# A hybrid trunk step on one core: spreading products, tile scaling, casts, first taps and score copies are placed differently

## The chip, the cores and the metric

The kernel runs on one core of a Trainium2 chip. A core has five engines, each with its own queue of instructions that runs in order: TensorE (PE, with its weight loads listed as PEld), VectorE (DVE), ScalarE (ACT), GpSimd (POOL) and SyncE (SP), which here only issues transfers. The metric is the device time of one launch in microseconds. Three runs of the kernel before took 1754.55, 1755.26 and 1755.8 us; the median is 1755.26 us.

## The reference

One layer of a hybrid trunk over 128 context and 256 latent tokens of width 2048, all in float32:

```python
mod = (jax.nn.silu(cond) @ p['w_mod'] + p['b_mod'])[:, None, :]
sh1, sc1, g1, sh2, sc2, g2 = jnp.split(mod, 6, axis=-1)
h = _rmsnorm(x, p['ln1_g']) * (1 + sc1) + sh1
z = h @ p['w_in']
q, k, v, cva, cvg, lx, lg = jnp.split(z, IN_SPLITS, axis=-1)
...
mix = jnp.concatenate([att.reshape(B, S, D_ATT), cv, rec], axis=-1) @ p['w_out']
x = x + g1 * mix
h = _rmsnorm(x, p['ln2_g']) * (1 + sc2) + sh2
u = _dwconv(h @ p['ffn_up'], p['ffn_conv_w'], p['ffn_conv_b'], FFN_CONV_WIDTH // 2, FFN_CONV_WIDTH // 2)
ug, uv = jnp.split(u, 2, axis=-1)
x = x + g2 * ((jax.nn.silu(ug) * uv) @ p['ffn_down'])
```

`att` is attention with 8 heads of 128 (context tokens read context; latent tokens read a window of latents with a bias, and a cached context). `cv` is a gated depthwise convolution of 31 taps with a LayerNorm and SiLU, `rec` a recurrence in two directions behind a convolution of 4 taps. A final RMSNorm ends the step.

## The kernel before, in words

**Products.** Every float32 matrix product is made of three products of rounded parts (`mm3`, L161 to L165): a weight piece of 128x1024 is loaded (`raw`), rounded on ACT (`whi`, L150), and the rest is taken on DVE (`wlo`, L152). There are 6 `raw` buffers and 3 each of `whi` and `wlo`. Sums of the large products go to 5 PSUM buffers (`mm_ps`), all others to 3 (`aux_ps`).

**The start** (`in_proj`, L529). x arrives transposed as 16 k-tiles of 128x384. Its squares are summed (`mean_squares`, products msq L505), and `norm_x` (L509) makes the factor 1/rms of each token: a sum and an addition on DVE, a power on POOL (L515), three diagonal matrices on DVE (L520), and three spreading products on PE (rx, L522) that put the factor of every token into all partitions. `scale(k, n)` (L523, L525) multiplies n k-tiles by it on DVE, reading rx. The modulation of a group of k-tiles comes from `mod_pair` (L244): products of w_mod chunks with the condition (modp, L271), a copy on ACT (L331), a transpose (modt, L334) and three or more small DVE operations into MC (L339 to L349). `modulate` (L471) then applies MC on ACT (`ht`, L477), rounds the tile on DVE (`hh`, L479) and takes the rest on DVE (`hl`, L480).

The k-tiles go in groups of 1, 1, 2, 4, 4 and 4 (`GROUPS`, numbered g = 0 to 5). In each group `proj_group` (L564) makes 20 output tiles; the first group's sums are copied on ACT (L584), later ones are added to z on DVE (L586), which also frees their PSUM buffer. The modulation of the next group runs beside it. For the groups that start at k-tile 8 and 12 (`mod_quad`, L279) a part is summed on DVE (L298, L300). In the kernel before, k-tile 0 is scaled at L537, and k-tiles 1 to 15 right behind the last operation of k-tile 0's `modulate` (`issue_after`, L549 to L551), in pieces of 3, 4, 4 and 4. `setup2` (L206, called in group 2) holds a short chain on DVE and one exponential on ACT (L214 to L230).

**Streams.** From `qkv` on, side work is cut into generators (`attention`, `conv_module`, `recurrent`, `mod_*`) that yield costs. Main products call `turn`, which advances each stream by its own rate; for attention it is 3.5 units for each 7.8 us of main work (AR, UNIT). `attention` (L677) for one head: mask (LAG0), then three score blocks, each of products S (L692 to L697), a scaled copy on DVE (L700 or L702 and L703), the maximum on DVE (L705), the exponential on ACT (L706), a reciprocal on DVE (L707) and a scaling on ACT (L708). Then it yields LAG1, transposes the blocks on PE (PTp, L719), copies them on ACT (L722, L724), multiplies by V (o, L727, L729) and copies the result on ACT (L731). `mod_cols` (L399) yields LAG1 too, between a copy and its transposes. `out_proj` (L867) drains what is left of the attention before its products with k-tiles 4 to 7 of the mixed heads (L886).

**Who sets the order.** The program's order gives priorities; a scheduler at build time places each engine's instructions by them and by what it takes to be ready, and may bring an instruction far forward. `high_priority` puts a block first, and `issue_after(i)` keeps a block's instructions on i's engine behind i.

Of the kernel before, what the change touches and what calls it, by code (L numbers as in the profile page):

```python
# [10 lines left out]
AF = mybir.ActivationFunctionType  # L11
ALU = mybir.AluOpType
# [11 lines left out]
SCALE = float(128 ** -0.5)  # L24
NEG = -1e30
CTX = 128
LAT = 256
T = CTX + LAT
TP = T + 2
NSLOT = 54  # L30
RAWB, HLB, MB, MMB, AUXB = 6, 3, 9, 5, 3
GROUPS = (1, 1, 2, 4, 4, 4)
# [8 lines left out]
CR, CV, AR = 2.5, 6, 3.5  # L41
MOD0, MOD1, MOD2 = 2.6, 1.3, .25

LAG0, LAG1, LAG2, LAG3 = 1, 1, 2, 3

RINGS = 4096

# [52 lines left out]
class Trunk:  # L100
# [140 lines left out]
        nc.gpsimd.dma_start(self.G[:, 3072:4096], I["cache_k"])  # L241


    def mod_pair(self, k0, kt):  # L244

        nc, tc = self.nc, self.tc
        pm = self.aux_ps("modp")
        parts = 1 if kt == 1 else 2
        w = kt * P // parts
        nk = 4 // kt  # L250
        wm = self.I["w_mod"]
        chunks = []
        n = KT // nk
        ends = bursts(n) if kt > 1 else list(range(1, n + 1))
        done = 0
        for i in range(n + PLAG):
            if i < n:
                v = self.misc("rawm")
                nc.sync.dma_start(v, wm[4 * k0 + i])
                chunks.append(v.rearrange("p (v k c) -> p v k c", v=2, k=nk))  # L260
                yield nk / KT
            if i + 1 - PLAG in ends:

                with tc.high_priority():
                    for m in reversed(range(done, i + 1 - PLAG)):
                        for k in range(nk):
                            for j in range(2 * parts):
                                vv, half = divmod(j, parts)
                                if parts == 1:
                                    j += 2 * (k % 2)  # L270
                                self.pair = nc.tensor.matmul(  # L271
                                    pm[32 * j:32 * j + 32, :w], lhsT=self.cT[:, m * nk + k, :],
                                    rhs=chunks[m][:, vv, k, half * w:(half + 1) * w],
                                    start=m == ends[0] - 1 and k < 3 - parts, stop=m == ends[-2] and k > nk - 4 + parts)
                done = i + 1 - PLAG
        with tc.high_priority():
            self.mod_pair_cols(k0, kt, w, parts, pm)

# [189 lines left out]
            self.hold = ins  # L468
        return hi, lo

    def modulate(self, kt, x, a, b):  # L471

        nc = self.nc
        t = self.slot(T, "ht")
        hi, lo = self.slot(T, "hh", F32R), self.slot(T, "hl", F32R)
        for c, s0, s1 in SEG:
            nc.scalar.activation(t[:, s0:s1], x[:, s0:s1], AF.Identity, bias=self.MC[:, b, kt, c:c + 1],  # L477
                                 scale=self.MC[:, a, kt, c:c + 1])
        nc.vector.tensor_copy(hi, t)  # L479
        return hi, lo, nc.vector.tensor_tensor(lo, t, hi.bitcast(F32), ALU.subtract)  # L480


# [26 lines left out]
    def norm_x(self, X, pm):  # L509

        nc = self.nc
# [12 lines left out]
            x = X[:, k:k + n]  # L524
            return nc.vector.tensor_tensor(x, x, r.unsqueeze(1).broadcast_to([P, n, T]), ALU.mult)  # L525

        return scale

    def in_proj(self):  # L529
        nc, tc = self.nc, self.tc  # L530
        st = self.streams
        X = self.load_x()
        pm = self.mean_squares(X)
        st.add("pair", 0, self.mod_pair(0, GROUPS[0]))
        st.drain("pair")
        scale = self.norm_x(X, pm)
        scale(0, 1)  # L537
        self.z = {}
        self.h = []
        k0 = 0  # L540
        for g, kt in enumerate(GROUPS):
            with tc.high_priority():
                for k in range(k0, k0 + kt):
                    *h, ins = self.modulate(k, X[:, k], 1, 0)
                    self.h.append(h)
            if g == 0:

                self.hold = self.scaled = ins
                with tc.issue_after(ins.ins):  # L549
                    for k, n in ((1, 3), (4, 4), (8, 4), (12, 4)):  # L550
                        scale(k, n)  # L551
            if g == 2:
                mark = self.mp.tile([P, 2], F32, tag="mark", bufs=1, name="mark")
                with tc.issue_after(nc.gpsimd.tensor_copy(mark, self.MC[:, 0, k0, :]).ins):
# [122 lines left out]
    def attention(self, h):  # L677
# [8 lines left out]
        for i in range(3):  # L686
# [10 lines left out]
                nc.tensor.matmul(o[:, LAT:T], lhsT=ql, rhs=self.ckT[:, h, :], start=True, stop=True)  # L697
            s = self.slot(n, "s")
            if i == 0:
                nc.vector.tensor_scalar(s, S[:, :n], SCALE, None, ALU.mult)  # L700
            else:
                nc.vector.scalar_tensor_tensor(s[:, :LAT], S[:, :LAT], SCALE, bt[i - 1][:, ::-1], ALU.mult, ALU.add)  # L702
                nc.vector.tensor_scalar(s[:, LAT:], S[:, LAT:T], SCALE, None, ALU.mult)  # L703
            st = self.mp.tile([P, 4], F32, tag="st", bufs=6, name="st")
            nc.vector.tensor_reduce(st[:, 0:1], s, AX.X, ALU.max, negate=True)  # L705
            nc.scalar.activation(s, s, AF.Exp, bias=st[:, 0:1], accum_out=st[:, 1:2])  # L706
# [29 lines left out]
    def conv_module(self):  # L736
# [7 lines left out]
        for c in range(4):  # L744
            a, g = self.z[24 + c], self.z[28 + c]
            u = self.mp.tile([P, W], F32, tag="cu", bufs=2, name="cu")
            nc.vector.memset(u, 0.0)
            nc.vector.tensor_tensor(u[:, 15:15 + CTX], a[:, :CTX], g[:, :CTX], ALU.mult)
            nc.vector.tensor_tensor(u[:, 30 + CTX:30 + T], a[:, CTX:], g[:, CTX:], ALU.mult)
            acc = self.slot(N, "cacc")  # L750
            nc.vector.tensor_scalar(acc, u[:, 0:N], self.cvw[:, c:c + 1], self.cv_b[:, c:c + 1], ALU.mult, ALU.add)
            yield 1.0
            for w in range(1, 31):
                nc.vector.scalar_tensor_tensor(acc, u[:, w:w + N], self.cvw[:, 4 * w + c:4 * w + c + 1], acc,  # L754
# [37 lines left out]
    def recurrent(self):  # L792
# [4 lines left out]
        for c in range(4):  # L797
            x = self.z[32 + c]
            u = self.mp.tile([P, TP + 3], F32, tag="cu", bufs=2, name="lu")
            nc.vector.memset(u, 0.0)  # L800
            nc.scalar.copy(u[:, 2:2 + CTX], x[:, :CTX])
            nc.scalar.copy(u[:, 4 + CTX:4 + T], x[:, CTX:])
            xc = self.slot(TP, "xc")
            nc.vector.tensor_scalar(xc, u[:, 0:TP], self.lcw[:, c:c + 1], self.lcb[:, c:c + 1], ALU.mult, ALU.add)
            for w in range(1, 4):
                nc.vector.scalar_tensor_tensor(xc, u[:, w:w + TP], self.lcw[:, 4 * w + c:4 * w + c + 1], xc,
                                               ALU.mult, ALU.add)
# [414 lines left out]
```

## Time and profile before

| | us |
|---|---|
| median of 3 runs | 1755.26 |
| the profiled execution's own time | 1755.48 |
| its span, from first to last instruction | 1753.7 |
| TensorE busy | 1718.2 |
| VectorE busy | 1160.9 |
| ScalarE busy | 741.9 |
| GpSimd busy | 146.0 |

The profiled execution is one run; some 1.8 us lie outside its span. "Busy" counts an instruction from its start to its end; matmuls overlap in a pipeline, so that PE can be busy and still not at its peak. All times below are from the start of the span. Of the granted clock, 1.00 is TensorE's upper level of 2.4 GHz, and 0.50 the lower one of 1.2 GHz.

### The profile page before, as it was taken

The numbers are of one execution on the slowest core, as the hardware profiler recorded it, in microseconds if no ns is written. First come the engines' busy times: TensorE is split into PE (matmuls) and PEld (weight loads), VectorE is DVE, ScalarE is ACT, GpSimd is POOL, SyncE is SP. The second block draws the span as 40 slices with busy tenths as digits, with TensorE's granted clock in tenths as the row PEclk, the third lists the DMA queues.
The fourth block names the chain that finished last, engine by engine and source line by source line (L and its number), as shares of the span: only waits on it lengthen the run. The fifth ranks groups of instructions, "written<-read, shape, count | busy, mean of one in ns | idle before, by whom it ended". The sixth has DMA issues, their size and how long they took to land.

```text
span 1753.7 us, 25229 instructions
## 1 busy us (share of the span) xinstructions
PE 1718.2 (98%) x9935; PEld 1559.9 (89%) x9935; DVE 1160.9 (66%) x1663; ACT 741.9 (42%) x1176; POOL 146.0 (8%) x240
## 2 busy tenths in 40 slices
PE   6999999999999989999999999999999999999998
PEld 5789988779887989999989898998989899898987
DVE  5699799988697455569544545459754545448467
ACT  5223456774443335443424343342434333333434
POOL 0100101313522000001000000001000000000002
PEclk9999999999999999999999999999999999999999
DMA  9887869898687443347444343447434343644333
GB/s 380 300 312 286 230 212 285 252 329 284 141 275 265 152 171 122 126 151 252 144 126 127 120 133 120 133 139 242 135 121 132 113 137 124 234 134 126 123 127 112
DMA packets 192839, 325.57 MB, mean 186 GB/s; under 512 B 11360, under 2 KB 123872, under 8 KB 192208
## 3 DMA queue, kind: packets, MB, share of 16 engines
q1 hardware_dynamic: 179136, 277.97, 47.0%
q0 software_dynamic: 13440, 45.94, 10.1%
q8 instruction: 78, 1.28, 0.3%
q14 instruction: 41, 0.34, 0.1%
q10 hardware_dynamic: 144, 0.05, 0.0%
HBM read 316.54 MB, written 7.38 MB: 185 GB/s over the span
## 4 chain that ended last, share of the span: by engine, by line
PE 92%; DVE 3%; issue 2%; ACT 1%; DMA 1%; POOL 0%; DVEq 0%; SPq 0%; POOLq 0%; ACTq 0%
PE mmp L163 29%; PE mmp L165 28%; PE mmp L164 28%; PE modp L367 1%; PE modp L271 1%; DVE wlo L152 1%; DVE acc L390 1%; DMA rawm<-w_mod 1%; ACT whi L150 0%; PE modp L396 0%; DVE acc L300 0%; PE o L729 0%; PE modp L306 0%; DMA X<-x_T 0%; PE PTp L719 0%
## 5 line engine op out<-in xcount | busy, mean ns | idle before, releaser
L152 DVE TENSOR_TENSOR wlo<-raw,whi 128x1024 fp32r<-128x1024 f32 x371 | 451.5, 1221 | 439.5 <-ACT whi L150 435.1
L150 ACT CAST whi<-raw 128x1024 fp32r<-128x1024 f32 x371 | 387.6, 1047 | 651.8 <-PE mmp L164 351.8
L163 PE MATMUL mmp<-hh,whi 128*128 128x384 f32 x1904 | 645.9, 341 | 6.7 <-DVE hh L479 3.5
L164 PE MATMUL mmp<-hl,whi 128*128 128x384 f32 x1904 | 642.4, 338 | 0.5 <-DVE hl L480 0.5
L165 PE MATMUL mmp<-hh,wlo 128*128 128x384 f32 x1904 | 642.5, 338 | 0.0
L163 PEld LDWEIGHTS mmp<-hh,whi 128*128 128x128 f32 x1904 | 357.8, 188 | 15.3 <-DVE hh L479 4.4
L164 PEld LDWEIGHTS mmp<-hl,whi 128*128 128x128 f32 x1904 | 358.5, 188 | 4.2 <-issue 2.4
L165 PEld LDWEIGHTS mmp<-hh,wlo 128*128 128x128 f32 x1904 | 358.4, 188 | 3.7 <-issue 2.0
L164 PE MATMUL mmp<-wlo,gh 128*128 128x512 f32 x504 | 198.8, 394 | 0.0
L165 PE MATMUL mmp<-whi,gl 128*128 128x512 f32 x504 | 198.4, 394 | 0.0
L163 PE MATMUL mmp<-whi,gh 128*128 128x512 f32 x504 | 198.2, 394 | 0.0
L390 DVE SCALAR_TENSOR_TENSOR acc<-rawm,cT,acc 128x1024 f32<-128x1024 f32 x120 | 149.1, 1282 | 5.9 <-DMA rawm<-w_mod 5.9
L163 PEld LDWEIGHTS mmp<-whi,gh 128*128 128x128 f32 x504 | 94.7, 188 | 22.6 <-ACT cv L955 0.8
L165 PEld LDWEIGHTS mmp<-whi,gl 128*128 128x128 f32 x504 | 94.7, 188 | 22.2
L164 PEld LDWEIGHTS mmp<-wlo,gh 128*128 128x128 f32 x504 | 94.8, 188 | 21.8 <-DVE wlo L152 0.4
L951 ACT ACTIVATE cv<-mmp,fcb,fcw 128x384 f32<-128x384 f32 x88 | 59.3, 675 | 120.0 <-PE mmp L165 120.0
L959 DVE SCALAR_TENSOR_TENSOR cv<-mmp,fcw,cv 128x381 f32<-128x381 f32 x176 | 97.0, 608 | 0.0
L1089 DVE TENSOR_TENSOR Y<-mmp,Y 128x512 f32<-128x512 f32 x96 | 65.9, 687 | 40.4 <-PE mmp L165 38.4
L381 POOL DMA_DIRECT2D rawm<-w_mod x64 | 34.3, 537 | 630.9 <-PE modp L396 341.1
L754 DVE SCALAR_TENSOR_TENSOR cacc<-cu,cvw,cacc 128x399 f32<-128x399 f32 x120 | 75.5, 633 | 2.2
L586 DVE TENSOR_TENSOR z<-mmp,z 128x384 f32<-128x384 f32 x100 | 52.3, 551 | 22.3 <-PE mmp L165 22.0
L955 ACT ACTIVATE cv<-mmp,cv,fcw 128x1 f32<-128x1 f32 x176 | 52.3, 350 | 1.4
(459 smaller groups left out, 1600.7 us busy)
## 6 DMA issues: line engine op xcount, KB each, us to landing
raw<-ffn_up SPq DMA_DIRECT2D x176, 512.0 KB, 3.5
rawm<-w_mod SPq DMA_DIRECT2D x128, 512.0 KB, 6.6
raw<-ffn_down SPq DMA_DIRECT2D x84, 512.0 KB, 3.6
raw<-w_in SPq DMA_DIRECT2D x72, 512.0 KB, 7.0
rawm<-w_mod POOLq DMA_DIRECT2D x64, 512.0 KB, 5.4
raw<-w_out SPq DMA_DIRECT2D x32, 512.0 KB, 4.9
raw<-w_in SPq DMA_DIRECT2D x14, 256.0 KB, 6.8
X<-x_T SPq DMA_DIRECT2D x4, 768.0 KB, 6.9
```

Source lines behind the costliest of these rows:

```text
L150: nc.scalar.copy(hi, raw)
L152: nc.vector.tensor_tensor(lo, raw, hi.bitcast(F32), ALU.subtract)
L163: mm(out, lhsT=a[0], rhs=b[0], start=start, stop=False)
L164: mm(out, lhsT=a[0], rhs=b[1], start=False, stop=False)
L165: mm(out, lhsT=a[1], rhs=b[0], start=False, stop=stop)
L390: nc.vector.scalar_tensor_tensor(acc[c], raws[m], col, acc[c], ALU.mult, ALU.add)
L586: self.mark = nc.vector.tensor_tensor(self.z[f], pz[:, :T], self.z[f], ALU.add)
L754: nc.vector.scalar_tensor_tensor(acc, u[:, w:w + N], self.cvw[:, 4 * w + c:4 * w + c + 1], acc, ALU.mult, ALU.add)
L951: nc.scalar.activation(t, p, AF.Identity, bias=self.fcb[:, f:f + 1], scale=w[1])
L955: nc.scalar.activation(t[:, d:d + 1], p[:, r:r + 1], AF.Identity, bias=t[:, d:d + 1], scale=w[i])
L959: nc.vector.scalar_tensor_tensor(tv[:, :, d], pv[:, :, s], w[i], tv[:, :, d], ALU.mult, ALU.add)
L1089: nc.vector.tensor_tensor(y, p, y, ALU.add)
```

## The change

`LAG1` becomes 2 where it was 1. `mod_pair` takes a function that it calls once, when all of its chunks but the last have had their products; the first group's gets `norm_x`, so the spreading products stand in the program before the last chunk's products, and their `issue_after(self.pair.ins)` points at the last product so far. Of the scaling, k-tiles 1 to 3 stay in group 0 behind k-tile 0; k-tiles 4 to 7 are scaled in group 1 and 8 to 15 in group 2, two at a time and without `issue_after`. From group 3 on (12 k-tiles) the rounding of a tile is done on ACT. The scaled copies of scores that need no bias (one of 128x128 in each of the 24 blocks) go to ACT. In the convolution and the recurrence the buffer's clearing is cut to its three gaps, and the first tap goes to ACT.

```diff
@@ -41,7 +41,7 @@
 CR, CV, AR = 2.5, 6, 3.5
 MOD0, MOD1, MOD2 = 2.6, 1.3, .25
 
-LAG0, LAG1, LAG2, LAG3 = 1, 1, 2, 3
+LAG0, LAG1, LAG2, LAG3 = 1, 2, 2, 3
 
 RINGS = 4096
 
@@ -241,7 +241,7 @@
         nc.gpsimd.dma_start(self.G[:, 3072:4096], I["cache_k"])
 
 
-    def mod_pair(self, k0, kt):
+    def mod_pair(self, k0, kt, between=None):
 
         nc, tc = self.nc, self.tc
         pm = self.aux_ps("modp")
@@ -273,6 +273,8 @@
                                     rhs=chunks[m][:, vv, k, half * w:(half + 1) * w],
                                     start=m == ends[0] - 1 and k < 3 - parts, stop=m == ends[-2] and k > nk - 4 + parts)
                 done = i + 1 - PLAG
+                if between and done == n - 1:
+                    between()
         with tc.high_priority():
             self.mod_pair_cols(k0, kt, w, parts, pm)
 
@@ -468,7 +470,7 @@
             self.hold = ins
         return hi, lo
 
-    def modulate(self, kt, x, a, b):
+    def modulate(self, kt, x, a, b, own=False):
 
         nc = self.nc
         t = self.slot(T, "ht")
@@ -476,7 +478,10 @@
         for c, s0, s1 in SEG:
             nc.scalar.activation(t[:, s0:s1], x[:, s0:s1], AF.Identity, bias=self.MC[:, b, kt, c:c + 1],
                                  scale=self.MC[:, a, kt, c:c + 1])
-        nc.vector.tensor_copy(hi, t)
+        if own:
+            nc.scalar.copy(hi, t)
+        else:
+            nc.vector.tensor_copy(hi, t)
         return hi, lo, nc.vector.tensor_tensor(lo, t, hi.bitcast(F32), ALU.subtract)
 
 
@@ -524,16 +529,18 @@
             x = X[:, k:k + n]
             return nc.vector.tensor_tensor(x, x, r.unsqueeze(1).broadcast_to([P, n, T]), ALU.mult)
 
-        return scale
+        self.scale = scale
 
     def in_proj(self):
         nc, tc = self.nc, self.tc
         st = self.streams
         X = self.load_x()
         pm = self.mean_squares(X)
-        st.add("pair", 0, self.mod_pair(0, GROUPS[0]))
+        self.pair = None
+        pair = self.mod_pair(0, GROUPS[0], lambda: self.norm_x(X, pm))
+        st.add("pair", 0, pair)
         st.drain("pair")
-        scale = self.norm_x(X, pm)
+        scale = self.scale
         scale(0, 1)
         self.z = {}
         self.h = []
@@ -541,14 +548,17 @@
         for g, kt in enumerate(GROUPS):
             with tc.high_priority():
                 for k in range(k0, k0 + kt):
-                    *h, ins = self.modulate(k, X[:, k], 1, 0)
+                    *h, ins = self.modulate(k, X[:, k], 1, 0, g > 2)
                     self.h.append(h)
             if g == 0:
 
                 self.hold = self.scaled = ins
                 with tc.issue_after(ins.ins):
-                    for k, n in ((1, 3), (4, 4), (8, 4), (12, 4)):
-                        scale(k, n)
+                    scale(1, 3)
+            if g in (1, 2):
+
+                for k in ((4, 6), (8, 10, 12, 14))[g - 1]:
+                    scale(k, 2)
             if g == 2:
                 mark = self.mp.tile([P, 2], F32, tag="mark", bufs=1, name="mark")
                 with tc.issue_after(nc.gpsimd.tensor_copy(mark, self.MC[:, 0, k0, :]).ins):
@@ -697,10 +707,10 @@
                 nc.tensor.matmul(o[:, LAT:T], lhsT=ql, rhs=self.ckT[:, h, :], start=True, stop=True)
             s = self.slot(n, "s")
             if i == 0:
-                nc.vector.tensor_scalar(s, S[:, :n], SCALE, None, ALU.mult)
+                nc.scalar.activation(s, S[:, :n], AF.Copy, scale=SCALE)
             else:
                 nc.vector.scalar_tensor_tensor(s[:, :LAT], S[:, :LAT], SCALE, bt[i - 1][:, ::-1], ALU.mult, ALU.add)
-                nc.vector.tensor_scalar(s[:, LAT:], S[:, LAT:T], SCALE, None, ALU.mult)
+                nc.scalar.activation(s[:, LAT:], S[:, LAT:T], AF.Copy, scale=SCALE)
             st = self.mp.tile([P, 4], F32, tag="st", bufs=6, name="st")
             nc.vector.tensor_reduce(st[:, 0:1], s, AX.X, ALU.max, negate=True)
             nc.scalar.activation(s, s, AF.Exp, bias=st[:, 0:1], accum_out=st[:, 1:2])
@@ -744,11 +754,12 @@
         for c in range(4):
             a, g = self.z[24 + c], self.z[28 + c]
             u = self.mp.tile([P, W], F32, tag="cu", bufs=2, name="cu")
-            nc.vector.memset(u, 0.0)
+            for s0 in (0, 15 + CTX, 30 + T):
+                nc.vector.memset(u[:, s0:s0 + 15], 0.0)
             nc.vector.tensor_tensor(u[:, 15:15 + CTX], a[:, :CTX], g[:, :CTX], ALU.mult)
             nc.vector.tensor_tensor(u[:, 30 + CTX:30 + T], a[:, CTX:], g[:, CTX:], ALU.mult)
             acc = self.slot(N, "cacc")
-            nc.vector.tensor_scalar(acc, u[:, 0:N], self.cvw[:, c:c + 1], self.cv_b[:, c:c + 1], ALU.mult, ALU.add)
+            nc.scalar.activation(acc, u[:, 0:N], AF.Identity, bias=self.cv_b[:, c:c + 1], scale=self.cvw[:, c:c + 1])
             yield 1.0
             for w in range(1, 31):
                 nc.vector.scalar_tensor_tensor(acc, u[:, w:w + N], self.cvw[:, 4 * w + c:4 * w + c + 1], acc,
@@ -797,11 +808,12 @@
         for c in range(4):
             x = self.z[32 + c]
             u = self.mp.tile([P, TP + 3], F32, tag="cu", bufs=2, name="lu")
-            nc.vector.memset(u, 0.0)
+            for s0, s1 in ((0, 2), (2 + CTX, 4 + CTX), (4 + T, TP + 3)):
+                nc.vector.memset(u[:, s0:s1], 0.0)
             nc.scalar.copy(u[:, 2:2 + CTX], x[:, :CTX])
             nc.scalar.copy(u[:, 4 + CTX:4 + T], x[:, CTX:])
             xc = self.slot(TP, "xc")
-            nc.vector.tensor_scalar(xc, u[:, 0:TP], self.lcw[:, c:c + 1], self.lcb[:, c:c + 1], ALU.mult, ALU.add)
+            nc.scalar.activation(xc, u[:, 0:TP], AF.Identity, bias=self.lcb[:, c:c + 1], scale=self.lcw[:, c:c + 1])
             for w in range(1, 4):
                 nc.vector.scalar_tensor_tensor(xc, u[:, w:w + TP], self.lcw[:, 4 * w + c:4 * w + c + 1], xc,
                                                ALU.mult, ALU.add)
```

## Rows read from the trace of the kernel before

**Rows 1.** The page, busy time of the engines: us, share of the span, instructions.

```profile
PE 1718.2 (98%) x9935; PEld 1559.9 (89%) x9935; DVE 1160.9 (66%) x1663; ACT 741.9 (42%) x1176; POOL 146.0 (8%) x240
```

**Rows 2.** PE's waits, whole run: waiting line <- releaser: us, times, longest.

```profile
PE PTp L719 <- ACT s L708: 3.5, 4, 1.9
```

**Rows 3.** Stretches: us, busy of PE, PEld, DVE, ACT, POOL, PE's clock, DMA share, GB/s.

```profile
53.00:61.00 8.00, 6.12 (x33) 3.72 (x36) 6.52 (x14) 2.98 (x4) 5.52 (x7) 0.79 1.03 341
...
200.00:350.00 150.00, 149.67 (x998) 123.04 (x997) 139.89 (x262) 90.58 (x126) 25.81 (x46) 1.00 0.80 245
...
441.00:451.00 10.00, 7.95 (x38) 7.44 (x37) 10.00 (x17) 5.93 (x13) 6.93 (x8) 0.83 0.89 135
```

**Rows 4.** Timeline 16:23: start, us, instruction [idle before <- releaser].

```profile
19.93 0.88 PE L522 MATMUL rx<-diag,ones 128*128 128x128 f32 x6
...
20.84 0.55 DVE L525 TENSOR_TENSOR X<-X,rx 128x384 f32<-128x384 f32 x1
22.45 0.36 DVE L479 CAST hh<-ht 128x384 fp32r<-128x384 f32 x1 [1.05 <-ACT ht L477]
...
22.86 0.45 PE L163 MATMUL mmp<-hh,whi 128*128 128x384 f32 x1 [2.06 <-DVE hh L479]
```

**Rows 5.** Timeline of DVE, first far-forward operation, then 25:37.

```profile
1.47 0.42 DVE L747 MEMSET cu<- 128x429 f32 x1
...
33.66 1.75 DVE L525 TENSOR_TENSOR X<-X,rx 128x1536 f32<-128x1536 f32 x1
...
36.45 0.15 DVE L349 SCALAR_TENSOR_TENSOR MC<-MC,pcol 128x2 f32<-128x2 f32 x1
```

**Rows 6.** Timeline 37:43: the second k-tile, on ACT, DVE and PE.

```profile
37.37 1.28 ACT L215 ACT_TABLE_LOAD   x1
...
39.88 1.00 ACT L477 ACTIVATE ht<-X,MC 128x128 f32<-128x128 f32 x2
...
41.54 0.17 DVE L223 TENSOR_SCALAR acc<-acc 128x8 f32<-128x8 f32 x1
...
41.67 0.44 PE L163 MATMUL mmp<-hh,whi 128*128 128x384 f32 x1 [1.49 <-DVE hh L479]
```

**Rows 7.** Timeline of PE: the two waits for DVE's z behind groups 1 and 3.

```profile
56.54 0.44 PE L163 MATMUL mmp<-hh,whi 128*128 128x384 f32 x1 [1.86 <-DVE z L586]
...
113.42 0.44 PE L163 MATMUL mmp<-hh,whi 128*128 128x384 f32 x1 [1.09 <-DVE z L586]
```

**Rows 8.** Groups by shape: xcount | busy us, mean ns | idle before <- releaser.

```profile
L479 DVE CAST hh<-ht 128x384 fp32r<-128x384 f32 x32 | 11.5, 358 | 12.9 <-ACT ht L477 12.8
...
L171 ACT CAST gh<-cv 128x384 fp32r<-128x384 f32 x44 | 22.1, 512 | 43.4 <-DVE cv L994 43.4
```

**Rows 9.** The copies of line L722: ns min/median/max, first and last start.

```profile
L722 ACT COPY PC<-PTp x8: 240/261/270, 299.5 to 525.9; 128x128 f32<-128x128 f32 x8
```

**Rows 10.** Timeline 440:446, the fifth head: DVE, ACT and PE.

```profile
440.56 0.28 DVE L700 TENSOR_SCALAR s<-S 128x128 f32<-128x128 f32 x1
...
441.45 0.40 ACT L706 ACTIVATE s<-s,st 128x128 f32<-128x128 f32 x1 [6.03 <-DVE st L705]
...
445.51 0.55 PE L719 MATMUL PTp<-ident,s 128*128 128x128 f32 x3 [1.87 <-ACT s L708]
```

**Rows 11.** Timeline 520:541, the last head on PE and ACT.

```profile
520.42 0.59 PE L696 MATMUL S<-z,z 128*128 128x256 f32 x2
...
527.50 0.62 ACT L708 ACTIVATE s<-s,st 128x384 f32<-128x384 f32 x1 [0.95 <-DVE st L707]
...
533.60 0.58 PE L163 MATMUL mmp<-whi,mix4h 128*128 128x512 f32 x1
...
541.10 0.40 PE L163 MATMUL mmp<-whi,mix7h 128*128 128x512 f32 x1
541.33 0.39 PE L164 MATMUL mmp<-wlo,mix7h 128*128 128x512 f32 x1
```

**Rows 12.** ACT's waits from 280 to 540: us, times, longest.

```profile
ACT whi L150 <- PE mmp L164: 19.6, 10, 4.0
```

## The prediction

> **What bounds the kernel now.** I read the page's busy times first. PE is busy for 98% of the span and DVE and ACT far less [rows 1], so time can only come from places where PE stands still or runs at its lower clock. PE's list of waits then names those that an edit here can touch: transposes of scores that wait for ACT's scaled block, 3.5 us in four waits [rows 2]. The timelines add those of the first 115 us: 2.06 us before the first main product [rows 4], 1.49 us before the second k-tile [rows 6], 1.86 us behind group 1 and 1.09 us in group 3, where PE waits for DVE to free a PSUM buffer [rows 7]. Last come the stretches with the granted clock. Around the wait behind group 1 it is 0.79 over 8 us and around the last wait of the attention 0.83 over 10 us [rows 3]; some 3.4 us of each were at the lower level, which takes (1 - 0.79) x 8 = 1.7 us and (1 - 0.83) x 10 = 1.7 us. All this together is 3.5 + 2.1 + 1.5 + 1.9 + 1.1 + 3.4 = 13.5 us: no more is within reach. The sum below is made against the profiled execution's 1755.5 us; the median of the three runs, 1755.26, is 0.2 us lower. A difference of under 0.2%, 3.5 us, counts as none.
>
> **Spreading products earlier: 0.** Their 0.88 us of PE [rows 4] stay. The last chunk's products have high priority and their data is there, while the diagonals hang on a power on POOL; I expect PE's queue to hold the same order. If they do go ahead, k-tile 0 is scaled up to 0.9 earlier, but its modulation comes up to 0.9 later, and both are needed. Ends: -0.9 and +0.9. Nothing else moves with `norm_x`: five small operations of DVE, one of POOL, no transfer.
>
> **Scaling in pieces of two: +0.9.** Four tiles take 1.75 [rows 5], one 0.55 [rows 4], so two take 0.55 + 1.2 / 3 = 0.95, six of them 5.7. Before, the pieces of later tiles could not pass k-tile 0; the new ones can, for nothing holds them, and DVE's queue takes what is ready: a buffer of the convolution is cleared at 1.47 us [rows 5], 200 us before its use, and a step of `setup2` stands between `hh` and `hl` of the second tile [rows 6]. So one piece falls into DVE's idle 1.05 before the first `hh` [rows 4], which costs nothing, and I expect a second one between `hh` and `hl`, which holds up the rest of k-tile 0 and the first `wlo` by 0.9. PE can't make that up, since the first group fills it. Ends: 0, and 5.7 - 1.05 = +4.7 if all six go first.
>
> **The second k-tile: -1.5.** Its last modulation step comes at 36.45 behind a piece of 1.75 that started at 33.66 [rows 5]. Then a table load for `setup2` stands ahead of its `ht`, which starts only at 39.88 [rows 6]. With two pieces gone by 23 us and the others half as long, the step comes some 2 us earlier and `ht` passes the table load. The wait of 1.49 goes; what is late next is DVE's sums of group 1. Ends: 0 and -1.5.
>
> **Behind group 1: -0.9.** The wait of 1.86 [rows 7] is DVE's backlog of the whole stage, with 20 sums of a tile, each about the 0.55 of a pass over 384 columns [rows 4]. Two pieces (1.9) pulled out of DVE's work, less the 0.9 they cost, leave about half the wait. Ends: -1.9 and 0. For the 1.7 us of clock behind it I take nothing, as a wait stays: ends -1.7 and +1.7.
>
> **Casts on ACT: -1.0.** A cast of 128x384 takes 0.36 on DVE and 0.51 on ACT [rows 8]. Group 3 has four, so DVE is 1.4 us ahead at 113.42, and the wait of 1.09 [rows 7] all but goes. ACT gets 12 x 0.51 = 6.1 us in the stages where it has to make `ht` and `whi` in turn. Ends: -1.1, and +1.8 if the longer cast lies on the path each time, 12 x (0.51 - 0.36). A sentence on the rule against this: the Trainium skill, "ScalarE: Activation LUTs", section "Rules for kernel authors", wants additions and products on VectorE and not on ScalarE. By that rule the term would be that +1.8 and the sum 2.8 us worse.
>
> **First taps, clearing: 0.** DVE loses eight first taps (at most 0.55 each, its pass over 384 columns [rows 4]) and eight clearings of about 0.42 [rows 5], and gets 24 very short ones. That lies where PE is busy 149.67 of 150 us [rows 3]: main products hide it. If that cover went, DVE would wait for eight taps on ACT of 0.51, +4.1; the other end is the 0.3 that PE is idle there.
>
> **Score copies: 0.** A copy of 128x128 takes 0.28 on DVE [rows 10] and 0.26 on ACT [rows 9], so 24 of them are 6.7 us less on DVE and 6.2 more on ACT. Each block gets one more hand-over, to ACT and back for the maximum; behind that maximum stand in DVE's queue the `wlo` that PE needs. As long as ACT is idle when a block comes (6.03 us before one of them [rows 10]) this hides behind main products; if not, it is the third rival.
>
> **One unit more before the transposes: -3.5 and -1.7.** A unit of the stream is 7.8 / 3.5 = 2.2 us of main work, and the longest of the four waits is 1.87 [rows 10], so all 3.5 us [rows 2] are covered, and the 1.7 us of clock, which follow the longest, go with them. What was late is DVE: the first copy of that head started at 440.56 [rows 10]. Ends: 0 and -5.2. The transposes of `mod_cols`, too, come 2.2 us of work later; nothing waits for them there.
>
> **The end of the attention and the new order: +1.8.** A head now costs 10 units, not 9. I counted yields against turns: at the drain before the products with heads 4 to 7, one step (o) of the last head was left, and now all of its transposes and o are, and its last score block comes three quarters of 7.8, 5.9 us, later. The scores of that block started at 520.42 and were scaled at 528.1 [rows 11]; now at about 526.3 and 534. From there to the last head's products is at least 4.5 us. PE is at the drain's products from some 531 us on (533.60 [rows 11] less the last head's steps, which now come later). Each is three matmuls 0.23 apart (541.10 to 541.33 [rows 11]), and 18 of those 24 don't need the last head: 18 x 3 x 0.23 = 12.4 us. So it is covered if PE's queue puts them first, as it has them now, with the last head's at 541.10. I charge two new waits of the mean size of the old ones, 3.5 / 4 = 0.9, one here and one anywhere else in the new order. Ends: 0 and +4.5.
>
> **Sum:** 0 + 0.9 - 1.5 - 0.9 - 1.0 + 0 + 0 - 3.5 - 1.7 + 1.8 = -5.9, so 1755.5 - 5.9 = **1749.6 us**.
>
> **Rivals.** First, *the change does not do what it says at the start*: the queue goes by readiness, so three pieces pass k-tile 0 (2.85 - 1.05 = +1.8), the second tile still gains its 1.5 and group 1 nothing. The start gives +0.3 in place of -1.5: 1751.4. For it speaks the buffer cleared at 1.47; against it, that high-priority work wins whenever it is ready. Second, *the attention's waits only move*: they are DVE's lag, and a later transpose meets a later lag; the terms -3.5 and -1.7 fall away: 1754.8. For it speaks that DVE is busy 10.00 of 10 us there [rows 3]; against it, that PE waited only four times, in eight heads. Third, on the other side, *ACT's queue holds the scores up*: between 280 and 540 us ACT stands 10 times, 19.6 us in all, for a weight buffer that PE has to free [rows 12], 1.96 each. A score copy queued behind such a wait makes DVE's maximum late, and with it DVE's next `wlo`, where DVE has no slack. With four of 24 blocks hit and nothing won in the attention it is 1754.8 + 4 x 1.96 = 1762.6; it decides from three blocks on, 1760.7. Against it: ACT's 6.03 us of idling. Fourth, *the casts lose*, +1.8 for -1.0: 1752.4. Fifth, *more goes than I count*: the rest of the wait behind group 1 (1.0) and its clock (1.7), and no new waits (1.8): 1745.1.
>
> **How the numbers follow.** I give the forecast 0.38 with a range of its own of 1746.5 to 1752, the rivals in their order 0.12, 0.20, 0.15, 0.08 and 0.07. Faster means under 1751.8: nearly all of the forecast (0.35), half of the first rival (0.06), the fifth (0.07) and a little of the fourth (0.02), 0.50. Slower means over 1758.8: the third and small parts of others, 0.17. The rest, 0.33, is the same. The range of 1744.5 to 1759 takes in all cases but most of the third rival and the ends of the others, under 0.2.
>
> **What the new profile would show.** Right: no wait for `hh` near 40 us; no PTp among PE's waits; clock 1.00 from 400 to 550 us; two-tile scalings on DVE, the first before `hh` and none longer than 1 us. Wrong: PE's first main product after 24 us (pieces first); DVE waiting for s on ACT some twenty times, with PE waiting for `wlo` (third rival); PTp's waits at other heads (second); PE waiting for the last head's products near 535 us.

## The result, and the profile after

The changed kernel takes 1765.35 us (median of four runs, 1764.81 to 1766.14) against 1754.9 for the kernel before (four runs as well): 1.0053 of its time, with a 95% interval of 1.0041 to 1.0066. The forecast was 1749.6, so the change loses 9.3 us by this ratio, 10.4 by the medians, where 5.9 were to be gained. The profiled execution took 1766.14 us with a span of 1764.3, against 1755.48 and 1753.7 before.

The page of the changed kernel, busy time of the engines (us, share, instructions):

```profile
PE 1722.9 (98%) x9935; PEld 1564.4 (89%) x9935; DVE 1150.5 (65%) x1638; ACT 755.9 (43%) x1219; POOL 147.2 (8%) x240
```

As meant, DVE is busy 10 us less and ACT 14 us more [rows 1]. PE's list of waits after (waiting line <- releaser: us, times, longest) shows where that went:

```profile
PE S L706 <- ACT s L713: 5.5, 1, 5.5
...
PE PTp L729 <- ACT s L718: 3.0, 2, 2.1
...
PE PTp L729 <- ACT PT L734: 1.7, 1, 1.7
```

The first line is new. The transposes' waits went from four to two and from 3.5 to 3.0 us [rows 2], and a new one of 1.7 stands at the drain. To place the loss in time I numbered the main products (L163 to L165) from 0 in both traces and compared the starts of those with the same number. The changed kernel is 0.6 us late at the first, 2.0 at number 80 (46.9 us before). Taken at every 40th product it is between 0.1 and 3.2 late up to number 1920 (there 1.0: 499.9 before, 500.9 after), 7.8 late at number 2000 and 10.0 at number 2040 (533.6 before). From there to the end it stays 9.5 to 10.7. So nearly all of it is lost between 500 and 545 us.

Stretches after, with the columns of [rows 3] (the second fence cuts out the time behind the wait):

```profile
53.00:61.00 8.00, 5.88 (x29) 4.39 (x27) 7.54 (x15) 3.95 (x6) 7.50 (x11) 0.98 1.02 389
41.00:46.00 5.00, 3.68 (x13) 3.43 (x14) 4.69 (x18) 1.86 (x3) 0.00 (x0) 0.77 0.94 356
441.00:451.00 10.00, 7.92 (x45) 7.62 (x44) 10.00 (x17) 5.08 (x13) 4.24 (x6) 0.94 0.70 84
200.00:350.00 150.00, 150.00 (x989) 123.95 (x991) 134.72 (x258) 97.64 (x141) 18.21 (x34) 1.00 0.79 248
500.00:512.00 12.00, 6.54 (x22) 4.97 (x21) 12.00 (x17) 3.59 (x9) 4.07 (x7) 0.72 0.94 178
```

```profile
507.00:509.00 2.00, 1.73 (x5) 1.55 (x6) 2.00 (x4) 1.94 (x5) 0.71 (x2) 0.50 1.14 151
509.00:511.00 2.00, 2.00 (x6) 1.52 (x6) 2.00 (x4) 0.93 (x3) 0.93 (x1) 0.50 0.57 152
511.00:513.00 2.00, 2.00 (x10) 1.60 (x9) 2.00 (x4) 1.11 (x2) 1.25 (x2) 0.93 0.91 335
```

The stretch of 500 to 512 us in the kernel before:

```profile
500.00:512.00 12.00, 12.00 (x59) 9.94 (x58) 12.00 (x13) 4.81 (x9) 3.58 (x6) 1.00 0.98 346
```

From 500 to 512 us PE is busy only 6.54 of 12 us and the granted clock is 0.72; the kernel before has PE busy for 12.00 us and a clock of 1.00 there. PE stood 5.46 us up to 507.27, and when it starts again the clock is 0.50, that is 1.2 GHz, up to some 511 us. From 507.27 to 513 that takes 0.5 x 1.73 + 0.5 x 2 + 0.07 x 2 = 2.0 us more. With the wait of 1.7 us at the drain it makes 5.5 + 2.0 + 1.7 = 9.2 us, and the products fall back by 10.0 - 1.0 = 9.0 between numbers 1920 and 2040 (the kernel before waits 0.9 us at the drain, at 537 us).

That wait on PE, and ACT and DVE at the same time (start, us, instruction [idle before <- releaser]):

```profile
496.81 0.60 PE L706 MATMUL S<-z,z 128*128 128x256 f32 x2
...
501.41 0.40 PE L165 MATMUL mmp<-whi,mix2l 128*128 128x512 f32 x1
507.27 1.22 PE L706 MATMUL S<-z,z 128*128 128x256 f32 x2 [5.46 <-ACT s L713]
```

```profile
497.66 0.28 ACT L710 ACTIVATE s<-S 128x128 f32<-128x128 f32 x1 [1.88 <-PE S L707]
506.56 0.40 ACT L716 ACTIVATE s<-s,st 128x128 f32<-128x128 f32 x1 [8.62 <-DVE st L715]
...
506.96 0.26 ACT L713 ACTIVATE s<-S 128x128 f32<-128x128 f32 x1
```

```profile
485.98 1.37 DVE L152 TENSOR_TENSOR wlo<-raw,whi 128x1024 fp32r<-128x1024 f32 x1
494.66 3.68 DVE L392 SCALAR_TENSOR_TENSOR acc<-rawm,cT,acc 128x1024 f32<-128x1024 f32 x3 [7.32 <-DMA rawm<-w_mod]
...
505.05 1.27 DVE L392 SCALAR_TENSOR_TENSOR acc<-rawm,cT,acc 128x1024 f32<-128x1024 f32 x1
506.25 0.28 DVE L715 TENSOR_REDUCE st<-s 128x1 f32<-128x128 f32 x1
506.45 0.41 DVE L712 SCALAR_TENSOR_TENSOR s<-S,bias 128x256 f32<-128x256 f32 x1
```

Read backwards. PE's last score block of the seventh head needs the PSUM buffer of its first two blocks, which ACT empties at 506.96 (L713). That copy stands behind an exponential, and this waits 8.62 us for DVE's maximum of the first block, which was copied at 497.66. DVE was not idle from 494.66 to 506.25. It worked off products of `mod_rows_dve` (L392), with rests of weight pieces (L152) and splits between them, because it had stood 7.32 us for a transfer of `w_mod`. The transfer is issued on POOL:

```profile
458.22 0.58 POOL L383 DMA_DIRECT2D rawm<-w_mod  x1
475.88 1.09 POOL L743 DMA_DIRECT2D out_new_k<-z  x2 [17.08 <-ACT z L650]
476.95 2.47 POOL L674 DMA_DIRECT2D bias<-na_bias  x4
483.25 0.36 POOL L683 TENSOR_SCALAR_AFFINE_SELECT bias<-bias 64x192 f32<-64x192 f32 x1 [3.83 <-DMA bias<-na_bias]
...
488.09 1.65 POOL L383 DMA_DIRECT2D rawm<-w_mod  x3
```

The two stores at 475.88 are the keys of the last two heads, whose projection ends only then. They were placed ahead of the bias loads and of the other `w_mod` loads, so POOL stood 17.08 us, and the masks that wait for the bias took the rest. The next three `w_mod` loads went out at 488.09. The same queue in the kernel before:

```profile
472.46 0.58 POOL L733 DMA_DIRECT2D out_new_k<-z  x1 [5.86 <-ACT z L640]
...
475.32 0.58 POOL L733 DMA_DIRECT2D out_new_k<-z  x1
475.89 1.59 POOL L381 DMA_DIRECT2D rawm<-w_mod  x3
```

There the bias loads (from 456.91 us) and five of the eight masks behind them stood ahead of the first store, POOL waited 5.86 us for it, and the three `w_mod` loads went out at 475.89. With the lag of two the scheduler that orders the queues put the same instructions into another order; nobody wrote that order.

### The profile page after: what moved, and what is told of

It is laid out like the page before. It is cut to its first block, busy times and chain, and to the rows that moved or that the text cites. A ratio compares the mean times of both kernels' runs of the same rounds, so it can differ in the third digit from the quotient of the medians.

```text
span 1764.3 us, 25264 instructions
## 1 busy us (share of the span) xinstructions
PE 1722.9 (98%) x9935; PEld 1564.4 (89%) x9935; DVE 1150.5 (65%) x1638; ACT 755.9 (43%) x1219; POOL 147.2 (8%) x240
## 4 chain that ended last, share of the span: by engine, by line
PE 69%; issue 2%; DVE 1%; DMA 1%; POOL 1%; ACT 0%; DVEq 0%; POOLq 0%; ACTq 0%
PE mmp L163 23%; PE mmp L165 23%; PE mmp L164 23%; DMA bias<-na_bias 1%; DVE acc L392 1%; DMA rawm<-w_mod 0%; DVE wlo L152 0%; PE modp L398 0%; PE xtp L467 0%; DMA raw<-ffn_down 0%; POOL bias L683 0%; POOL bias L684 0%; PE auxp L165 0%; PE auxp L163 0%; PE auxp L164 0%
## 5 line engine op out<-in xcount | busy, mean ns | idle before, releaser
L152 DVE TENSOR_TENSOR wlo<-raw,whi 128x1024 fp32r<-128x1024 f32 x371 | 451.8, 1222 | 441.6 <-ACT whi L150 437.3
L163 PE MATMUL mmp<-hh,whi 128*128 128x384 f32 x1904 | 646.8, 341 | 6.2 <-DVE hh L484 3.6
L165 PE MATMUL mmp<-hh,wlo 128*128 128x384 f32 x1904 | 642.4, 338 | 0.0
L163 PEld LDWEIGHTS mmp<-hh,whi 128*128 128x128 f32 x1904 | 358.7, 189 | 15.6 <-issue 4.6
L165 PEld LDWEIGHTS mmp<-hh,wlo 128*128 128x128 f32 x1904 | 358.4, 188 | 2.5 <-issue 1.2
L165 PE MATMUL mmp<-whi,gl 128*128 128x512 f32 x504 | 198.5, 394 | 0.0
L163 PE MATMUL mmp<-whi,gh 128*128 128x512 f32 x504 | 197.6, 393 | 0.0
L392 DVE SCALAR_TENSOR_TENSOR acc<-rawm,cT,acc 128x1024 f32<-128x1024 f32 x120 | 149.7, 1281 | 11.9 <-DMA rawm<-w_mod 11.9
L163 PEld LDWEIGHTS mmp<-whi,gh 128*128 128x128 f32 x504 | 94.7, 188 | 22.0 <-ACT cv L967 0.8
L165 PEld LDWEIGHTS mmp<-whi,gl 128*128 128x128 f32 x504 | 94.7, 188 | 21.7
```

What stands on the lines that cost most here:

```text
L152: nc.vector.tensor_tensor(lo, raw, hi.bitcast(F32), ALU.subtract)
L163: mm(out, lhsT=a[0], rhs=b[0], start=start, stop=False)
L165: mm(out, lhsT=a[1], rhs=b[0], start=False, stop=stop)
L392: nc.vector.scalar_tensor_tensor(acc[c], raws[m], col, acc[c], ALU.mult, ALU.add)
```

## The experiments

Theory A: POOL's queue is the cause. Theory B: the score copies on ACT are. Theory C: the longer lag itself is. Each kernel was timed beside the kernel before on the same chip; all ratios are to that.

**Late stores.** Only the two stores move, behind the last mask. In the two traces PE, DVE, ACT and SP do the same operations in the same order, and so does POOL but for the two stores.

```diff
-        nc.gpsimd.dma_start(self.O["new_k"][hs], k[:, :P])
+        if h < 6:
+            nc.gpsimd.dma_start(self.O["new_k"][hs], k[:, :P])
+        elif h == 7:
+            with self.tc.issue_after(self.masked.ins):
+                for j in (6, 7):
+                    nc.gpsimd.dma_start(self.O["new_k"][j * P:(j + 1) * P], self.z[8 + j][:, :P])
```

(`masked` is the last `affine_select` of L684.)

> The changed kernel, with only the two stores of the last two heads' keys put later in POOL's queue. Theory A (POOL's queue stands 17.1 us for the keys of heads 6 and 7 with w_mod transfers behind it, VectorE so gets its products late and stands 7.3 us, and the score buffers of head 6 come free 5.5 us late): the waits of 7.3 us and 5.5 us go, and with the 5.5 us the half clock of 6.8 us behind it; 1755 to 1758 us. Theory B (the score copies on ACT hold the buffers): no change, 1764 to 1766 us. Theory C (the longer lag itself, by putting the score blocks and transposes closer together): no change, 1763 to 1766 us.

Measured: 1.0004 [0.9995, 1.0013], 1756.18 us. The loss is gone, 0.0053 - 0.0004 = 0.49% or 8.6 us of it by two stores of 64 KB each that nothing in the kernel waits for. POOL and the stretch at 500 us in this run:

```profile
457.64 0.58 POOL L383 DMA_DIRECT2D rawm<-w_mod  x1
458.22 2.45 POOL L674 DMA_DIRECT2D bias<-na_bias  x4
...
470.19 1.65 POOL L383 DMA_DIRECT2D rawm<-w_mod  x3
```

```profile
500.00:512.00 12.00, 12.00 (x57) 9.79 (x56) 12.00 (x13) 5.20 (x9) 6.98 (x12) 1.00 0.68 230
```

The three loads go out 17.9 us earlier (488.09 to 470.19), the score block waits for nothing, and the clock is at its upper level. At main product 2000 this kernel is 3.3 us ahead of the kernel before, where the changed kernel is 7.8 behind. DVE's waits for `w_mod` from 200 to 545 us, changed kernel and late stores:

```profile
DVE acc L392 <- DMA rawm<-w_mod: 11.9, 3, 7.3
```

```profile
DVE acc L392 <- DMA rawm<-w_mod: 4.7, 1, 4.7
```

The wait that is left stands at 424.54 us; behind it DVE waits for no transfer of `w_mod` up to 545 us.

**Copies back on DVE.**

```diff
-                nc.scalar.activation(s, S[:, :n], AF.Copy, scale=SCALE)
+                nc.vector.tensor_scalar(s, S[:, :n], SCALE, None, ALU.mult)
...
-                nc.scalar.activation(s[:, LAT:], S[:, LAT:T], AF.Copy, scale=SCALE)
+                nc.vector.tensor_scalar(s[:, LAT:], S[:, LAT:T], SCALE, None, ALU.mult)
```

> The changed kernel with the score copies back on VectorE. Theory A: POOL's queue keeps its order, so 1763 to 1766 us and the wait of a score block at about 501 us stays. Theory B: the buffers are freed as before, 1756 to 1758 us. Theory C: 1763 to 1766 us.

Measured: 1.0052 [1.0040, 1.0064]. A score block waits 4.0 us for the same buffer, now emptied by DVE. Beside the longer lag the copies are not the cause: B falls for the change as it stands.

**Lag one**, on the changed kernel, and **only lag two**, on the kernel before:

```diff
-LAG0, LAG1, LAG2, LAG3 = 1, 2, 2, 3
+LAG0, LAG1, LAG2, LAG3 = 1, 1, 2, 3
```

> The changed kernel with the lag before the transposes back at one unit. Theory A: POOL's queue has the w_mod transfers ahead of the last bias blocks again, 1755 to 1758 us. Theory B: 1763 to 1766 us. Theory C: 1755 to 1758 us, with the transposes' waits of before (3.5 us by four) back.

> The kernel before with only the longer lag. Theory A: POOL's queue gets the changed kernel's order, and with it most of the loss: 1761 to 1764 us. Theory B: 1753 to 1756 us. Theory C: 1761 to 1764 us.

Measured: 1.0043 [1.0031, 1.0055] for lag one, where B's number came and those of A and C did not, and 1.0036 [1.0023, 1.0048] for only lag two, as A and C say. In the latter POOL stands 21.9 us for the two stores, and PE's wait is back:

```profile
501.34 0.70 PE L696 MATMUL S<-z,z 128*128 128x256 f32 x2 [4.58 <-DVE s L703]
```

So the longer lag alone makes most of the loss, 0.0036 of 0.0053. But with the lag taken back the change still loses, and there B is the better theory.

**Only lag two, late stores**, the kernel before with both edits above:

> The kernel before with the longer lag and the two late stores. Theory A (the longer lag gains what it was forecast to gain, and lost it only through POOL's queue): the products stay some 4 us ahead of the kernel before up to 490 us, the score block's wait of 4.6 us goes, and what is left of the loss is the 3 us at the drain: 1751 to 1755 us against 1756.1 for the kernel before. If the longer lag costs something besides POOL's queue at the end of attention: 1757 us or more.

Measured: 0.9987 [0.9978, 0.9996], 1754.92 against 1756.67 us. At main product 1880 (490.0 us before) it is 3.2 us ahead, where only lag two had been 4.2. No score block waits for its buffer. C falls: without the stores' place in the queue the longer lag costs nothing, and gains a little (the interval ends at 0.9996). At the drain the lead is lost: 3.9 us ahead at number 2000, 0.5 behind at 2080, and 0.4 ahead at the end of this execution.

**Late stores, factors spread after the drain.**

```diff
-        pair = self.mod_pair(0, GROUPS[0], lambda: self.norm_x(X, pm))
+        st.add("pair", 0, self.mod_pair(0, GROUPS[0]))
+        st.drain("pair")
+        self.norm_x(X, pm)
```

> The changed kernel with late stores, and the factors spread after the first modulation products as before. If the earlier spreading costs 0.6 us of wait at the first product and shifts the clock's half stretch at 43 us in (1.4 us): 1753.5 to 1755 us against 1756.2 with late stores alone, the first product at 22.9 us. If it costs nothing: 1756 us.

Measured: 0.9996 [0.9987, 1.0005], not told apart from late stores alone. The first product came at 23.5 us here too, not at 22.9. In the kernel with only the score copies moved, whose start is that of before, it came at 23.7. So the 0.6 us is within what the start varies by from one execution to another.

**Lag one, copies on DVE**, the changed kernel with both edits (what is left is the start, the casts, the taps), and **only the copies on ACT**, on the kernel before:

> The changed kernel with lag one and the score copies on VectorE, so the kernel before with the start, the casts and the first taps changed. If the score copies on ACT made the loss that stayed with lag one (1763.4): 1756.5 to 1759 us, the start's 2 us alone. If the start, the casts and the taps made it: 1762 to 1764 us.

> The kernel before with only the score copies on ACT. If the copies made the loss that stayed with lag one: 1759 to 1762 us, with transposes waiting over 3 us at 445 us. If not: 1755 to 1757 us.

Measured: 1.0007 [0.9998, 1.0016] and 1.0038 [1.0026, 1.0051]. What lag one had left was the copies. On their own they cost as much as the longer lag does; the whole change, which has both, costs 0.0053, less than their 0.0036 + 0.0038.

**Only the copies on ACT, late stores.**

> The kernel before with the score copies on ACT and the two late stores. If the copies' loss (6.6 us) came through POOL's queue as the longer lag's did: 1756 to 1757.5 us. If it comes from ACT's queue, where a copy stands behind an exponential that waits for VectorE's maximum: 1761.5 to 1764 us. If the stretch at 445 us is ACT's (3.4 us of lag there) and the one at 505 us POOL's (2 us): 1759 to 1761.5 us.

Measured: 1.0028 [1.0019, 1.0037], the third case. PE's wait near 509 us (1.75 us for a transpose) is gone, those near 445 stay. So the larger part of the copies' loss at lag one is not the two stores' doing; how large can't be said closely, as the two intervals overlap. The traces show less than the times: with the stores of before the products fall back by 3.3 us near 445 and 2.0 near 509, with late stores by 1.9 near 445, and what is lost behind 545 us (2.0 late at number 2200, 4.1 at the end) stays open. The fifth head in the run with only the copies on ACT, to be held against [rows 10]:

```profile
433.39 0.38 PE L692 MATMUL S<-z,z 128*128 128x128 f32 x2
```

```profile
438.54 0.28 ACT L700 ACTIVATE s<-S 128x128 f32<-128x128 f32 x1 [1.73 <-DVE mix12l L172]
443.68 0.40 ACT L706 ACTIVATE s<-s,st 128x128 f32<-128x128 f32 x1 [4.86 <-DVE st L705]
...
444.08 0.26 ACT L703 ACTIVATE s<-S 128x128 f32<-128x128 f32 x1
```

```profile
442.88 0.57 DVE L172 TENSOR_TENSOR mix15l<-z,mix15h 128x384 fp32r<-128x384 f32 x1
443.35 0.29 DVE L705 TENSOR_REDUCE st<-s 128x1 f32<-128x128 f32 x1
```

The copy is done by 438.8, but DVE takes the maximum only at 443.35, behind products of `w_mod` and the splits. The next block's copy (444.08) stands behind the exponential of the first, so that its maximum too is late. Counted from the head's first score, the first maximum comes 10.0 us after it, where it was 9.1 in the kernel before; the transposes of the second block come at 449.13, 15.7 us after it, where they were 13.5.

**Only the first copy on ACT**, and **only the later ones**: the first or the second of the two edits above, on the kernel before.

> The kernel before with only the first block's score copy on ACT. If the loss comes from the extra crossing ahead of the first maximum, which lets VectorE's queue put other work first: 1759 to 1763 us, with 8 us or more from the first score to its maximum in most heads. If it comes from the later copies standing behind an exponential in ACT's queue: 1755 to 1757.5 us.

> The kernel before with only the later blocks' score copies on ACT. If the loss comes from the crossing ahead of the first maximum: 1755 to 1757.5 us. If it comes from the later copies standing behind an exponential: 1759 to 1763 us.

Measured: 1.0017 [1.0009, 1.0026] and 1.0010 [1.0001, 1.0018]. The first copy costs 3.0 us by its ratio (between 1.6 and 4.6; the median, 1760.47, lies in the first forecast). In its run the first maximum comes 8.6 to 11.5 us after the first score in four of eight heads, not in most (10.1, 11.5, 8.6 and 9.7 in heads 0, 1, 2 and 4); before it was 1.9, 6.0, 3.7 and 9.1. The later ones stand at 1757.73 us, between the two forecasts, and cost 1.8 us by their ratio (0.2 to 3.2). Together the two make 0.0027 of the 0.0038, and the intervals leave room for a plain sum.

In heads 0 to 2 it is not DVE that is late. The copy itself starts 9.7, 10.1 and 7.4 us after the score, where DVE's came 1.4, 5.4 and 3.2 us after it: ACT is busy, mostly with table loads and functions of the recurrence (L820 to L832), and the copy stands in its queue behind them. In head 1 the score starts at 319.2 us and ACT has no pause until the copy:

```profile
328.77 0.62 ACT L829 ACTIVATE V<-V,sp 128x386 f32<-128x386 f32 x1
329.30 0.26 ACT L700 ACTIVATE s<-S 128x128 f32<-128x128 f32 x1
```

Only in head 4 is the copy early (4.8 us after the score, before 8.6) and DVE's maximum late, as the forecast has it. The main products lose nothing in heads 0 to 2 (1.6 us late at number 1120, 1.1 at 1400) and 1.2 us at head 4.

**Last head at lag one**, on only lag two with late stores, and on the change with late stores:

```diff
-        yield LAG1
+        yield LAG1 if h < 7 else 1
```

> The kernel before with the longer lag for heads 0 to 6 alone, lag one for the last head, and the two late stores. If the 4.4 us that the longer lag loses at the drain (530 to 540 us) come from the last head's transposes being left for the drain: 1750.5 to 1753 us against 1754.9 with lag two for all heads and 1756.7 for the kernel before. If the drain costs the same in another way: 1754 to 1756 us.

> The whole change, with the two late stores and lag one for the last head. If both repairs add up: 1753 to 1755 us against 1756.2 with the late stores alone; if the copies on ACT take the drain's gain: 1756 us.

Measured: 0.9995 [0.9986, 1.0003] and 0.9995 [0.9987, 1.0003]. Neither can be told from its kernel without the edit (0.9987 and 1.0004), and PE's wait at the drain stays in both (2.2 us for `mix4h`, 1.7 for PT). The last head's lag is not what the drain costs. The trace of only lag two, late stores accounts for most of its 4.4 us: PE waits 2.2 us for `mix4h` where it waited 0.9 (for `wlo`) before; the clock is 0.66 over 531 to 536 us (1.00 before), (1 - 0.66) x 5 = 1.7 us; the rest, about 1.4, is of the size of the attention's own products on PE that the longer lag had put off until then (1.4 us of them at number 2000). That last part is no loss: some of the lead before it was work not yet done.

**The good parts together**: the kernel before with lag two for heads 0 to 6, late stores, casts and first taps on ACT and the shorter clearing.

> The kernel before with the parts that looked good or free: lag two for heads 0 to 6, the casts and the first taps on ACT, the shorter clearing, and the two late stores; the score copies and the whole start are those of before. If the casts gain the 0.9 us by which the products move up at 113 us: about 1 us below the same without them; 1750 to 1752.5 us.

Measured: 1.0003 [0.9995, 1.0012], a miss: no gain over the same without casts and taps (0.9995). The lowest ratio of all is that of the kernel before with lag two and late stores, 0.9987 or 2.3 us under it, less than the 0.2% that the prediction counts as a difference, and not clear of the 0.9995 of the two kernels above.

## Why the prediction was wrong

**The step that failed** is *the end of the attention and the new order, +1.8*, with its ends of 0 and +4.5. It charged two new waits of the mean size of the old ones. The runs show one wait of 5.5 us with 2.0 us of clock behind it, and 1.7 us at the drain, 9.2 in all. It failed because the working followed PE, ACT and DVE through the longer lag but not POOL's queue. The stores of the keys and the bias loads are issued from the same stream as the transposes, so a longer lag moves them as well, and `w_mod` loads of another stream stand behind them. The price was to be read from the trace of before: POOL waited there 5.86 us for one of these stores. Moving the two stores alone brings 8.6 us back.

**One unit more before the transposes, -3.5 and -1.7:** right in part. With lag two and late stores PE waits 1.9 us for the transposes where it waited 3.5 [rows 2]. The longest wait, at 445 us, is DVE's backlog and stays with a later transpose, as the second rival said of all of them (1.88 us at 445.29; in the changed kernel 2.08 at 449.36; before 1.87 [rows 10]). The clock behind it stays as well: 0.83 over 441 to 451 us with lag two and late stores, as before [rows 3], and in the changed kernel the half stretch begins only near 450 (0.66 over 449 to 454). So of 5.2 us 1.6 are seen to go. The three terms of the lag, -3.5 - 1.7 + 1.8 = -3.4, stand against 1756 x -0.0013 = -2.3 us (between -3.9 and -0.7) with late stores, and +6.3 without; that -2.3 comes near -3.4 is in part luck.

**Score copies, 0:** wrong, +6.7 us (1756 x 0.0038) when made alone. The argument was that ACT is idle when a block comes, and it was read from one block. In heads 0 to 2 ACT is busy and the copy comes 7.4 to 10.1 us after the score, but the main products hide that. In the seventh head of the changed kernel ACT is idle, 8.62 us long, but for DVE's maximum, in front of a copy that is ready. Where time is lost, at the fifth head, the copy was done 4.5 us before DVE took its maximum: a crossing (a hand-over between engines) behind which DVE's queue had other work first. The way from that head's first score to the transposes grew by 2.2 us, 0.9 of them at this maximum; that the later crossings made the rest is read from the rows, no run separates them. The third rival, *ACT's queue holds the scores up*, priced a loss of this size, 1762.6 us, and had the place right for three heads, but another reason: ACT waiting for PE to free a weight buffer. Those waits fell, from 19.6 us [rows 12] to 14.0 with only the copies and 10.3 in the whole change. With lag two and late stores the copies cost little: the whole change then stands at 1.0004 and lag two alone at 0.9987, and of the 0.0017 between them the start, the casts and the taps make 0.0007 by their own run; the rest is within the intervals.

**Casts on ACT, -1.0:** right in the profile. The casts took 512 ns on ACT and 360 on DVE, and yet the wait of 1.09 us [rows 7] went and the products came up by 0.9 us there (2.8 late at number 320, 1.9 at 360). The Trainium skill, "ScalarE: Activation LUTs", section "Rules for kernel authors", wants additions and products on VectorE; the row does not name casts, and read for them too, as the prediction read it, it would have made the term +1.8. The trace agrees that one cast is shorter on DVE, not on the outcome, since DVE was the engine that PE waited for. In the time of a whole run the 0.9 can't be seen.

**First taps, clearing, 0:** right in the outcome. PE is busy 150.00 of 150 us there; the taps on ACT were longer than the 0.51 us assumed, 713 and 708 ns each in the two kinds.

**Scaling in pieces, +0.9; the second k-tile, -1.5; behind group 1, -0.9:** all three wrong, with one cause. No piece went ahead of k-tile 0:

```profile
18.52 1.51 PE L527 MATMUL rx<-diag,ones 128*128 128x128 f32 x6
19.96 0.64 PE L271 MATMUL modp<-rawm,cT 128*32 128x128 f32 x16
...
23.45 1.01 PE L163 MATMUL mmp<-hh,whi 128*128 128x384 f32 x2 [2.06 <-DVE hh L484]
```

```profile
26.17 4.81 DVE L530 TENSOR_TENSOR X<-X,rx 128x1152 f32<-128x1152 f32 x5
...
34.15 0.94 DVE L530 TENSOR_TENSOR X<-X,rx 128x768 f32<-128x768 f32 x1
...
35.09 0.94 DVE L530 TENSOR_TENSOR X<-X,rx 128x768 f32<-128x768 f32 x1
```

```profile
38.27 1.28 ACT L215 ACT_TABLE_LOAD   x1
...
40.41 0.99 ACT L479 ACTIVATE ht<-X,MC 128x128 f32<-128x128 f32 x2
```

```profile
42.17 0.44 PE L163 MATMUL mmp<-hh,whi 128*128 128x384 f32 x1 [1.50 <-DVE hh L484]
```

```profile
58.51 0.44 PE L163 MATMUL mmp<-hh,whi 128*128 128x384 f32 x1 [1.83 <-DVE z L596]
```

Five scalings run in one go after `hl`, the last two just ahead of the second modulation step, so the table load still comes first. The waits are 1.50 and 1.83 us where they were 1.49 [rows 6] and 1.86 [rows 7]. The size of a piece was right (0.94 for 0.95). **Spreading products earlier, 0:** the order was not the one expected, as `rx` does go ahead of the last 16 products, but the time is. The start, the casts and the taps together measure +1.2 us (between -0.4 and +2.8), where the prediction had -2.5 (0.9 - 1.5 - 0.9 - 1.0).

## What to carry to other kernels

Where several streams share an engine's queue, a lag that moves one stream moves all that it issues, stores and loads included: list for each queue what now stands behind an instruction that waits, and who is fed by it. A store that nobody waits for belongs behind the loads that someone waits for, or it makes them late by its own wait. Before a small operation is moved off a busy engine, count the crossings on its chain, and read the other engine's queue at every place where the operation will stand, not at one: here 6.7 us of work saved on DVE cost 6.7 us of time, where DVE had to take the result back.

## What was not expected of the hardware

Two stores that move nothing urgent cost 8.6 us through their place in a queue alone: POOL stood 17.08 us for their data with loads behind them. The Trainium skill, "Trainium Kernel Development and Optimization", section "Key Constraints", says that issuing from several queues only saves the sequencer's issue time; no run here issues the stores from another queue, but the runs show that within one queue the order decided when the loads behind a store could start.

In the first 65 us the clock's half stretches differ between kernels with nearly the same waits. In the changed kernel there is one at 43.7 us (0.77 over 41 to 46), just behind the wait of 1.50 us. The kernel before, with a wait of 1.49 us there, has none (clock 1.00 over the same stretch). Behind group 1 both have one (0.83 over 56 to 66 us in each); it begins later in the changed kernel (0.98 over 53 to 61 us, before 0.79 [rows 3]). The same near 445 us: with late stores PE waits 2.25 us at 447.48 and the clock is 1.00 over 441 to 451, while the changed kernel, with the same order on PE, waits 2.08 us and has a half stretch behind it. So a wait of that length is followed by a half stretch in some runs and not in others, and a term of 1.7 us for it can't be told in advance from the wait alone.
